# The product with w_in in seven half products, on a normed stream kept on chip as seven blocks

## The chip, the cores and the metric

The kernel runs on one core of one Trainium2 chip. The metric is the device time of one launch in microseconds (us). Every float32 product is made on TensorE (PE) from two rounded halves of each operand, a high part `hi` and a low remainder `lo`, as three matmuls: hi by hi, hi by lo, lo by hi.

## The reference

One encoder block over 1040 positions (16 learned meta tokens ahead of 1024 frames) of width 1024. Eight heads stand side by side: heads 0 to 3 are mLSTM heads, heads 4 to 7 retention heads. Each needs q and k (128 wide), v and an output gate o (256 wide), and all are columns of one product with `w_in`.

```python
up   = rmsnorm(h, norm_mix_g)                  # h: meta tokens and x, 1040 x 1024
proj = up @ w_in                               # 1024 x 6152
q, k = silu(causal_dwconv(...)) or rotary(...) # per head, 128 wide
h_ml = sigmoid(ml_o) * head_norm(mlstm_chunkwise(q, k, v, gates))
h_rt = silu(rt_g)    * head_norm(retention_chunkwise(q, k, v))
h = h + concat(h_ml, h_rt) @ w_out             # 2048 x 1024
h = h + channel_mixer(rmsnorm(h, norm_ffn_g))  # w_up, w_gate, conv, w_down; 2816 wide
out = rmsnorm(h, norm_final_g)[16:]
```

## The kernel before, in words

Activations lie with the features on the partitions: 8 blocks (`KB`) of 128 features by 1040 positions. The code is traced once in Python, fully unrolled; a planner then orders the instructions of each engine by its own costs, by data dependences and by hand-written order edges (`after`). Semaphores are made from that.

**The stream.** `resid` (8 blocks, float32) is loaded once and stays on chip for the whole kernel. `gained` multiplies it by the norm's gain and splits it into `uh` and `ul`, four pieces of positions at a time (`NP`). The 1/rms of each position is not multiplied in there: it is applied where a product is taken out of PSUM, as `Rb` (a row per position) for q, k and o, and as `Rc`, `Rg`, `Rk` (a column per position) for v and in the scan. So PE can start before the norm of a piece is known.

**The product with w_in.** It goes head by head in the order `HEADS` = 4, 0, 1, 2, 3, 5, 6, 7. Weights come as units of 128 x 1024 (or 1056 for the first v): `issue` (L129) loads a unit by SP's queue into one of two raw buffers, ACT makes `hi` (L145) and DVE `lo` (L146), in one of three buffers; `need` asks for a unit and two ahead of it.

- `v_group` (L411 to 434) makes v with positions on the partitions, one chunk of 128 positions at a time: 8 blocks x 3 matmuls of 256 columns (L431 to 433). The 16 meta positions are a small float32 product of their own (L420). `v_evac` writes `vh` and `vl` (L406, L407).
- `fm_mms` (L436 to 443) makes q, k and the two halves of o with features on the partitions, in three pieces of 400, 384 and 256 positions. `qk_group` finishes a piece of q or k on the way out of PSUM: a convolution of four taps and SiLU for mLSTM heads (L462 to 468), the rotation for retention heads (L470 to 473). `o_group` (L483, L484) applies the sigmoid or SiLU.
- `gates` works the gate rows of all mLSTM heads out once, after head 4's v; `tables` brings them, or the rotation's tables, into `A1` and `A2`.

**The scan.** Each head runs over nine chunks (16 positions, then eight times 128): `scan_a` (L842 on) makes scores, `scan_b` (L882 on) the chunk's output and the carried state, `post_steps` the head's norm and the product with the gate. These pieces are laid by `merge` between the products of the same head's o and the next head's v:

```python
for i, h in enumerate(HEADS):
    merge([... o_group(h, b, p) ...], [A(0)] + [B(c) for c in range(4 if i < 7 else NCH)])
    ...
    merge([lambda c=c: v_group(g, c)() for c in range(NCH)], side)   # g: the next head
    tables(g)
    for kind in "qk":
        for p in range(3):
            qk_group(g, kind, p)
```

**After it.** The products with `w_out`, `w_up`, `w_gate` and `w_down` are each made in seven half products in place of eight already (`Seven`, `seven`), in which sums of weight quarters and of activation blocks stand for the quarters themselves. For `w_out` those sums are made on DVE by `wsum` (L185) during heads 1 to 7 and stored to DRAM; for `w_down` by `dload`, `dsum` and `dstep` (L198 to 234), on DVE, during the products with w_up and w_gate. Two positions at the end of the sequence fall outside the halves; `last_two` (L173) adds their share of w_out on DVE into `acc` (L178).

PSUM has eight banks: three `pp`, two `sA`, and one each of `num`, `upd` and `tr`.

Of the kernel before, what the change touches and what calls it, by code (L numbers as in the profile page):

```python
# [35 lines left out]
UN = 4 * 264  # L36
# [6 lines left out]
FIRST = HEADS[0]  # L43
PIECES = [(0, 400, (0, 1, 2, 3)), (400, 784, (4, 5, 6)), (784, 1040, (7, 8))]
WMAX = 400
# [19 lines left out]
def body(ctx, tc, h_in, vecs, cst, mask_in, rot, w_v0, w_v, w_fm, w_out, w_up, w_gate, w_down, out):  # L65
# [9 lines left out]

    def after(later, first):

        tc.add_manual_dep(later.ins, first.ins.name, mybir.DependencyInfo(mybir.DependencyClass.NoSync, mybir.DependencyReason.DATA),
                          reason="order")
# [5 lines left out]
    resid = per.tile([P, KB, T], F32, name="resid")  # L85
    upool = ctx.enter_context(tc.tile_pool(name="upool", bufs=1))
    ublk = [tuple(upool.tile([P, 2 * T], F32R, tag=f"u{x}{i}", name=f"u{x}{i}") for x in "hl") for i in range(4)]
    uh, ul = ([ublk[kb // 2][x][:, (kb % 2) * T:(kb % 2 + 1) * T] for kb in range(KB)] for x in (0, 1))
    accseg = ExitStack()
    accp = accseg.enter_context(tc.tile_pool(name="accp", bufs=1, side="right"))  # L90

    acc = accp.tile([P, 2, D], F32, name="acc")
    mm = accp.tile([P, 2 * 8, 2], F32, name="mm")
    rring = []
# [3 lines left out]
    epsc = per.tile([P, 1], F32, name="epsc")  # L98
    Rb = per.tile([P, T], F32, name="Rb")

    ident = cs[:, C_ID:C_ID + P]

    NP = [(0, 144), (144, 400), (400, 784), (784, 1040)]
    nc.scalar.dma_start(vec, vecs)
    for kb in (0, 4):
        nc.sync.dma_start(resid[:, kb:kb + 4, 0:144], h_in[:, kb:kb + 4, 0:144])
    nc.vector.memset(epsc, EPS)
    nc.scalar.activation(Rb[:, 0:1], epsc, AF.Square)

    PSB = {"pp": 3, "sA": 2, "num": 1, "upd": 1, "tr": 1}  # L110

    def pp(name, tag="pp"):
        return ps.tile([P, 512], F32, tag=tag, name=name, bufs=PSB[tag])

# [5 lines left out]
    def unit(key, src, n):  # L120
        units.append((key, src, n))
# [7 lines left out]
    def issue(upto):  # L129
        while issued[0] < min(upto, len(units)):  # L130
            u = units[issued[0]]
            issued[0] += 1
            if callable(u[1]):
                ready[u[0]] = u[1]()
                continue
            key, src, n = u
            nm = "_".join(str(k) for k in key)
            raw = raw_tile(nm)
            sub = 2 if key[:2] == ("v", FIRST) else 1
            cuts = [n * i // sub for i in range(sub + 1)]  # L140
            for c0, c1 in zip(cuts, cuts[1:]):
                nc.sync.dma_start(raw[:, c0:c1], src[:, c0:c1])
            hi, lo = split_tiles(nm)
            for c0, c1 in zip(cuts, cuts[1:]):
                x = (nc.scalar.copy(hi[:, c0:c1], raw[:, c0:c1]),  # L145
                     nc.vector.tensor_tensor(lo[:, c0:c1], raw[:, c0:c1], hi[:, c0:c1].bitcast(F32), ALU.subtract))  # L146
                if key[:2] in (("k", FIRST), ("o", FIRST)):
                    for a, b in zip(x, last["evac"]):
                        after(a, b)
            ready[key] = (hi, lo, raw)  # L150
# [8 lines left out]


    def u_v(h):
        for half in range(2):
            if h == FIRST:
                unit(("v", h, half), w_v0[half], 4 * 264)
            else:
                unit(("v", h, half), w_v[h - (h > FIRST), half], 4 * 256)

    def u_f(h, kind):
        j = {"q": 0, "k": 1, "o": 2}[kind]
        for b in range(2 if kind == "o" else 1):  # L170
            unit((kind, h, b), w_fm[h, j + b], D)

    def last_two(k, raw=None):  # L173
        raw = raw_tile(f"m{k}") if raw is None else raw
        nc.sync.dma_start(raw[:, :D], w_out[k])
        for t in range(2):
            if k != 2 * FIRST:
                nc.vector.scalar_tensor_tensor(acc[:, t], raw[:, :D], mm[:, k, t:t + 1], acc[:, t], ALU.mult, ALU.add)  # L178
            else:
                nc.vector.tensor_scalar(acc[:, t], raw[:, :D], mm[:, k, t:t + 1], None, ALU.mult)  # L180


    sums = {(g, st, k): dram.tile([P, 2 * HB], F32, name=f"ws{g}{st}_{k}") for g, n in (("w", 8), ("d", KD)) for st in ("65", "73") for k in range(n)}

    def wsum(g, k):  # L185
        src, n = (w_out, 8) if g == "w" else (w_down, KD)
        a, b = (accp.tile([P, 2 * HB], F32, tag=f"rr{i}", name=f"ws{g}{k}_{i}") for i in range(2))
        nc.sync.dma_start(a, src[k])
        nc.sync.dma_start(b, src[k + n])
        w11, w21, w12, w22 = a[:, :HB], a[:, HB:], b[:, :HB], b[:, HB:]  # L190
        after(nc.vector.tensor_tensor(w22, w21, w22, ALU.add), last["qk"])
        nc.vector.tensor_tensor(w21, w21, w11, ALU.subtract)
        nc.vector.tensor_tensor(w11, w22, w11, ALU.subtract)
        nc.vector.tensor_tensor(w12, w12, w11, ALU.subtract)
        for st, i, x in (("65", 0, w11), ("65", 1, w22), ("73", 0, w12), ("73", 1, w21)):
            nc.sync.dma_start(sums[g, st, k][:, i * HB:(i + 1) * HB], x)

    def dload(k, q, x):  # L198

        n = HB // 2  # L200
        b = x.rearrange("p (a b j) -> p a b j", a=2, b=2)
        for i in range(2):
            nc.sync.dma_start(b[:, :, i], w_down[k + i * KD].rearrange("p (a j) -> p a j", a=2)[:, :, q * n:(q + 1) * n])

    def dsum(k, q, x, prev):

        n = HB // 2
        w11, w12, w21, w22 = (x[:, i * n:(i + 1) * n] for i in range(4))
        after(V.tensor_tensor(w22, w21, w22, ALU.add), prev)
        V.tensor_tensor(w21, w21, w11, ALU.subtract)  # L210
        V.tensor_tensor(w11, w22, w11, ALU.subtract)
        V.tensor_tensor(w12, w12, w11, ALU.subtract)
        for st, i, j in (("65", 0, 4), ("73", 1, 3)):
            nc.sync.dma_start(sums["d", st, k].rearrange("p (a j) -> p a j", a=2)[:, :, q * n:(q + 1) * n],
                              x.rearrange("p (i j) -> p i j", i=4)[:, i:j:3 if st == "65" else 1])

    dcount = [0, 0]
    dunits = [(k, q) for k in range(KD) for q in range(2)]
    dbufs = []

    def dnext():

        if len(dunits) > dcount[1]:
            x = dbufs[dcount[1] % 2] or fp4.tile([P, 2 * HB], F32, tag="dsum", name=f"dsum{dcount[1]}", bufs=1)
            dopen.append((*dunits[dcount[1]], x))
            dload(*dopen[-1])
            dcount[1] += 1

    dopen = []

    def dstep(x):
        if dopen:
            dsum(*dopen.pop(0), x)
            dnext()


# [4 lines left out]
    def first_right(k):  # L241
        a = accp.tile([P, 2 * HB], F32, tag="rr0", name=f"fr{k}")
        r = accp.tile([P, 2 * HB], F32R, tag="rr1", name=f"frs{k}")
        nc.sync.dma_start(a, mxd[k])
        nc.scalar.copy(r[:, :HB], a[:, :HB])
        after(nc.vector.tensor_tensor(r[:, HB:], a[:, :HB], r[:, :HB].bitcast(F32), ALU.subtract), last["qk"])
        nc.vector.tensor_tensor(a[:, HB:], a[:, HB:], a[:, :HB], ALU.subtract)
        nc.sync.dma_start(rone[k], r.bitcast(F32))
        nc.sync.dma_start(diff[k], a[:, HB:])

    ahead = {(g, "q", 0): [lambda k=k: wsum("w", k)] for k, g in enumerate((1, 2, 3, 5, 6, 7))}
    for k, g in ((6, 6), (7, 7)):
        ahead[g, "k", 1] = [lambda k=k: wsum("w", k)]
    for k in range(8):
        ahead[5 + k // 3, *(("q", 1), ("q", 2), ("k", 0))[k % 3]] = [lambda k=k: first_right(k)]

    def u_m(h):
        for b in range(2):
            units.append((("m", h, b), lambda k=2 * h + b: last_two(k)))

    def u_vqk(h):
        u_v(h)
        u_f(h, "q")
        u_f(h, "k")

    u_vqk(FIRST)
    for i, h in enumerate(HEADS):
        u_f(h, "o")
        if i:
            u_m(HEADS[i - 1])  # L270
        if i < 7:
            u_vqk(HEADS[i + 1])


# [57 lines left out]
    def gained(kb, t0, t1, gcol, dve=False):  # L332
        g = vec[:, gcol + kb:gcol + kb + 1]
        if dve:
            nc.vector.tensor_scalar(uh[kb][:, t0:t1], resid[:, kb, t0:t1], g, None, ALU.mult)
        else:
            nc.scalar.activation(uh[kb][:, t0:t1], resid[:, kb, t0:t1], AF.Copy, scale=g)
# [234 lines left out]
    def tables(h):  # L572
        if h > H + 1:
            return
# [16 lines left out]

    HALF = SEQ // 2
    QT = HALF // 2  # L600

# [1082 lines left out]
```

## Time and profile before

| | us |
|---|---|
| median of 3 runs | 1538.67 (1537.11 to 1539.1) |
| span of the profiled execution | 1536.0 |
| busy in it: PE, DVE, ACT, POOL | 1512.7, 1131.5, 743.2, 2.5 |
| product with w_in and the scans | about 0 to 690 of the span |
| product with w_out | about 690 to 870 |
| products with w_up and w_gate | about 870 to 1305 |
| product with w_down and the last norm | about 1305 to 1536 |

The profiled execution has no time of its own beside its span; the span runs from the first to the last instruction, and the median of the runs lies 2.7 us above it. In a row of a group of instructions stand line, engine, operation, output and inputs, shape and count, then busy time, mean nanoseconds of one, and the idle time before it with what ended it. PEld is the loading of weights into PE, beside its matmuls. A line such as L146 is a line of the kernel before.

### The profile page before, as it was taken

The page shows a single profiled execution, that of the slowest core. Times are in us where ns is not written, and L with a number is a line of the kernel's source. Part 1 is how long each engine was busy: PE and PEld are TensorE (multiplying, and loading weights), DVE is VectorE, ACT ScalarE, POOL GpSimd, SP SyncE. Part 2 cuts the span into 40 slices and gives each one's busy share as a digit, 9 for nine tenths or more (in the row PEclk, how much of TensorE's full clock was granted, in tenths as well). Part 3 has the DMA queues.
Part 4 walks back from the last instruction along what each step waited for, and adds up shares of the span by engine and source line. Part 5 has one row for each costly group of instructions (what it writes and reads, how often), then busy time and mean ns, then how long its engine had stood idle before and what let it go on. Part 6 is the DMA issues. An engine that isn't in the chain of part 4 may idle for free.

```text
span 1536.0 us, 25538 instructions
## 1 busy us (share of the span) xinstructions
PE 1512.7 (98%) x9753; PEld 1392.8 (91%) x9753; DVE 1131.5 (74%) x2443; ACT 743.2 (48%) x1491; POOL 2.5 (0%) x13
## 2 busy tenths in 40 slices
PE   7999999999999999999999999999999999999997
PEld 7989999999999999998788998999999999888887
DVE  8757767686867677687966788677777777778657
ACT  7374555555542534434454465444444444344443
POOL 0000000000000000000000000000000000000000
PEclk9999999999999999999999999999999999999999
DMA  6131231332425346278542245323465656933313
GB/s 216 42 98 63 70 122 65 109 112 80 141 67 184 126 131 209 91 249 305 184 146 97 83 129 181 102 93 101 155 193 167 198 186 230 366 109 104 96 42 111
DMA packets 111771, 213.18 MB, mean 139 GB/s; under 512 B 9944, under 2 KB 54688, under 8 KB 111648
## 3 DMA queue, kind: packets, MB, share of 16 engines
q1 hardware_dynamic: 111504, 211.48, 41.8%
q8 instruction: 76, 1.25, 0.3%
q14 instruction: 47, 0.39, 0.1%
q10 hardware_dynamic: 144, 0.07, 0.0%
HBM read 155.89 MB, written 55.62 MB: 138 GB/s over the span
## 4 chain that ended last, share of the span: by engine, by line
PE 95%; DMA 2%; DVE 2%; ACT 1%; issue 0%; DVEq 0%; ACTq 0%
PE pv L431 4%; PE pv L432 4%; PE pv L433 4%; PE po L442 4%; PE po L441 4%; PE po L443 4%; PE pdx L608 3%; PE pdx L610 3%; PE pdx L609 3%; PE pup_x L609 2%; PE pup_x L610 2%; PE pga_x L608 2%; PE pga_x L610 2%; PE pga_x L609 2%; PE pup_x L608 2%; PE pdy L608 2%
## 5 line engine op out<-in xcount | busy, mean ns | idle before, releaser
L431 PE MATMUL pv<-hi_v,uh 128*128 128x256 f32 (+1 forms) x512 | 147.2, 288 | 7.7 <-ACT hi_v L145 7.7
L432 PE MATMUL pv<-lo_v,uh 128*128 128x256 f32 (+1 forms) x512 | 145.9, 286 | 0.0
L433 PE MATMUL pv<-hi_v,ul 128*128 128x256 f32 (+1 forms) x512 | 145.6, 285 | 0.0
L441 PE MATMUL po<-uh,hi_o 128*128 128x386 f32 (+2 forms) x384 | 125.1, 326 | 0.0
L442 PE MATMUL po<-ul,hi_o 128*128 128x386 f32 (+2 forms) x384 | 122.8, 320 | 0.0
L443 PE MATMUL po<-uh,lo_o 128*128 128x386 f32 (+2 forms) x384 | 122.6, 319 | 0.0
L431 PEld LDWEIGHTS pv<-hi_v,uh 128*128 128x128 f32 x512 | 97.2, 190 | 10.5 <-ACT hi_v L145 7.7
L432 PEld LDWEIGHTS pv<-lo_v,uh 128*128 128x128 f32 x512 | 96.9, 190 | 0.9 <-DVE lo_v L146 0.8
L433 PEld LDWEIGHTS pv<-hi_v,ul 128*128 128x128 f32 x512 | 96.9, 190 | 0.1
L299 ACT CAST hi_up<-raw_up 128x512 fp32r<-128x512 f32 (+1 forms) x52 | 36.5, 719 | 105.7 <-PE pga_z L609 60.7
L441 PEld LDWEIGHTS po<-uh,hi_o 128*128 128x128 f32 x384 | 72.5, 189 | 0.1
L442 PEld LDWEIGHTS po<-ul,hi_o 128*128 128x128 f32 x384 | 72.4, 189 | 0.1
L443 PEld LDWEIGHTS po<-uh,lo_o 128*128 128x128 f32 x384 | 72.2, 188 | 0.1
L608 PE MATMUL pup_x<-uh_g,hi_up 128*128 128x256 f32 (+1 forms) x240 | 67.2, 282 | 0.4 <-ACT uh_g L1096 0.4
L609 PE MATMUL pup_x<-ul_g,hi_up 128*128 128x256 f32 (+1 forms) x240 | 67.4, 283 | 0.1
L610 PE MATMUL pup_x<-uh_g,lo_up 128*128 128x256 f32 (+1 forms) x240 | 66.3, 282 | 0.0
L300 DVE TENSOR_TENSOR lo_ga<-fraw_ga,hi_ga 128x512 fp32r<-128x512 f32 (+1 forms) x52 | 41.9, 808 | 32.2 <-ACT hi_ga L299 32.1
L300 DVE TENSOR_TENSOR lo_d<-rd,hi_d 128x1024 fp32r<-128x1024 f32 (+1 forms) x34 | 37.7, 1112 | 34.8 <-ACT hi_d L299 34.8
L441 PE MATMUL pq<-uh,hi_q 128*128 128x400 f32 (+2 forms) x192 | 62.1, 323 | 1.0 <-DVE qT L472 0.9
L442 PE MATMUL pk<-ul,hi_k 128*128 128x400 f32 (+2 forms) x192 | 62.1, 324 | 0.0
L441 PE MATMUL pk<-uh,hi_k 128*128 128x400 f32 (+2 forms) x192 | 62.0, 323 | 0.0
L443 PE MATMUL pq<-uh,lo_q 128*128 128x400 f32 (+2 forms) x192 | 62.0, 323 | 0.0
(757 smaller groups left out, 4978.7 us busy)
## 6 DMA issues: line engine op xcount, KB each, us to landing
raw_up<-w_up_d SPq DMA_DIRECT2D x22, 512.0 KB, 3.6
fraw_ga<-w_gate_d SPq DMA_DIRECT2D x22, 512.0 KB, 4.5
acts<-cv SPq DMA_DIRECT2D x44, 256.0 KB, 3.5
rd<-wsd SPq DMA_DIRECT2D x22, 512.0 KB, 3.5
raw_o<-w_fm_d SPq DMA_DIRECT2D x16, 512.0 KB, 3.5
wsw<-w_out_d SPq DMA_DIRECT2D x16, 512.0 KB, 3.8
wsw<-wsw SPq DMA_DIRECT2D x32, 256.0 KB, 2.1
raw_v<-w_v_d SPq DMA_DIRECT2D x14, 512.0 KB, 3.7
```

Of the source, the lines that this page charges most:

```text
L299: nc.scalar.copy(hi[:, o:o + n], x)
L300: nc.vector.tensor_tensor(lo[:, o:o + n], x, hi[:, o:o + n].bitcast(F32), ALU.subtract)
L431: nc.tensor.matmul(pv[:L, :nv], a, hi[:, o:o + nv], start=kb == 0, stop=False)
L432: nc.tensor.matmul(pv[:L, :nv], a, lo[:, o:o + nv], start=False, stop=False)
L433: nc.tensor.matmul(pv[:L, :nv], b, hi[:, o:o + nv], start=False, stop=kb == KB - 1)
L441: nc.tensor.matmul(pt[:, :n], a, uh[kb][:, t0:t1], start=kb == 0, stop=False)
L442: nc.tensor.matmul(pt[:, :n], a, ul[kb][:, t0:t1], start=False, stop=False)
L443: nc.tensor.matmul(pt[:, :n], b, uh[kb][:, t0:t1], start=False, stop=kb == KB - 1)
L608: m.append(nc.tensor.matmul(pt, ah, xh_, start=first and k == 0, stop=False, skip_group_check=True))
L609: nc.tensor.matmul(pt, ah, xl_, start=False, stop=False, skip_group_check=True)
L610: m.append(nc.tensor.matmul(pt, al, xh_, start=False, stop=last and k == n - 1, skip_group_check=True))
```

## The change

The product with w_in is put into seven half products, like the four others. Its input features are halved (4 blocks each), its output columns are halved, and the positions are halved into two stretches of `SB` = 528 (the second begins at position 512, so 16 positions are made twice). With X11 to X22 the four blocks of the normed stream (position half, feature half) and S1 to S4 sums of them, each of seven products takes one block and one quarter, or sum of quarters, of the weights.

```diff
+    ROWS = [("x", "11", 0, 0), ("y", "12", 0, 1), ("x", "S2", 1, 0), ("y", "S1", 1, 1), ("x", "S3", 2, 1), ("y", "S4", 3, 0), ("x", "22", 2, 0)]
+    def wino_fm(kind, h, chunks, dst):
+        get = gbanks(f"{kind}{h}")
...
+        for n, (b, xb_, ui, hf) in enumerate(ROWS):
+            for ci, (j0, j1) in enumerate(chunks):
...
+                    hi, lo, _ = need((kind, h, ui), 2)
...
+                    mm3s(pt, [tuple(x[:, hf * HB + k * P:hf * HB + (k + 1) * P] for x in (hi, lo)) for k in range(4)],
+                         [tuple(x[:, k, j0:j1] for x in u) for k in range(4)], n in (0, 1, 3), n in (1, 5, 6))
...
+                    if n in (0, 6):
+                        nc.scalar.copy(d, q)
+                    elif n in (2, 3):
+                        nc.scalar.activation(d, q, AF.Copy, scale=-1.0)
+                    else:
+                        last["pace"] = V.tensor_tensor(d, d, q, ALU.add if n == 1 else ALU.subtract)
...
+    FMC = [(0, 264), (264, SB)]
+    OC = [(KEEP, 272), (272, SB)]
```

q and k of a head are the two column halves of one group (`qk_steps`), the two halves of o of another (`o_steps`). v is made for two heads of `PAIRS` = (0, 1), (2, 3), (5, 6) in one group (`v_steps`: four pairs of 128 positions, 256 columns each); head 7's v is a group with features on the partitions (`v7_steps`) and is transposed back per chunk (`v_split`). Head 4, the first, keeps v, q and k as plain products (`v4_group`, `q4_group`); its o is a group. q and k land as `raws`, and `qk_final` does the convolution or rotation from there; v stays in float32 and `v_split` splits it into `hi` and `lo` chunk by chunk, in the scan.

The stream is normed before it is split. `first_norm` takes five stretches in turn; after the last, the sums are made in place of blocks that are no longer needed:

```diff
+        for i, x in enumerate(xs):
+            for k in range(4):
+                V.scalar_tensor_tensor(x[:, k], x[:, k], vec[:, V_MIX + 4 * i + k:V_MIX + 4 * i + k + 1], pr, ALU.mult, ALU.mult)
+            h_, l_ = (u[:, :, j0:j1] for u in UB[f"{half + 1}{i + 1}"])
+            nc.scalar.copy(h_, x)
+            last["pace"] = V.tensor_tensor(l_, x, h_.bitcast(F32), ALU.subtract)
...
+    usum(0, "22", "21", "S1")
+    usum(0, "11", "21", "21")
+    usplit("S3", "21", "r0", "r1")
+    usum(1, "S1", "11", "11")
+    usum(1, "11", "12", "12")
+    usplit("S4", "12", "r2", "r3")
+    usplit("S2", "11", "uh2", "ul2")
+    usplit("S1", "S1", "uh3", "ul3")
```

The seven blocks fill the room of `resid`; so x is loaded a second time, ahead of the product with w_out, into `RT`.

Sums of weight quarters are made in DRAM by adding DMAs of POOL's queue (GpSimd's), for w_in (`insum`), w_out and w_down (`wsum`), in place of DVE's sums; `job` issues an insum at the start of each group, two groups ahead of its use. `last_two` scales on ACT and adds into DRAM:

```diff
+    def wsum(g, k):
...
+        for x, y in ((d65, src[k]), (d73[:, HB:], v21), (d73[:, :HB], v12)):
+            dep(G.dma_start(x, y), last["pace"], True)
+        add(d65[:, HB:], v22)
+        add(d73[:, HB:], v11)
+        add(d65[:, :HB], d65[:, HB:])
+        add(d73[:, :HB], d65[:, :HB])
+    def insum(w, q, n, cuts):
+        for i in range(cuts):
+            c = 4 * n // cuts
+            dep(G.dma_start(q[:, i * c:(i + 1) * c], w[:, i * c:(i + 1) * c]), last["pace"], True)
+        b = lambda x, o: x[:, o * n:(o + 1) * n]
+        add(b(q, 1), b(w, 3))
+        add(b(q, 3), b(w, 0))
+        add(b(q, 0), b(q, 1))
+        add(b(q, 2), b(q, 0))
...
+            nc.scalar.activation(x, raw, AF.Copy, scale=mm[:, k, t:t + 1])
...
+                G.dma_start(accd[t], x, accum_op=ALU.add)
```

The order around it: each group of products (`group`) takes some of the scan's pieces of the head before.

```diff
+    for p, (a, b) in enumerate(PAIRS):
+        group(qk_steps(a), 7)
+        steps, meta = v_steps(p)
+        group(steps[:12], 99, 0, 10)
+        tables_load(a)
+        meta()
+        qk_final(a)
+        tables_make(a)
+        side += tasks(a)
+        if p:
+            wsum("w", wjobs.pop(0))
+        merge(steps[12:], take(5), 6)
+        group(o_steps(a), 5)
...
+        group(qk_steps(b), 99)
...
+        qk_final(b)
+        tables_make(b)
+        side += tasks(b)
+        group(o_steps(b), 5, 5)
```

The banks of PSUM become two `pa`, two `pb` and one each of `sA`, `num`, `upd` and `tr`. Signs of the sums in the later products are turned so that DMAs need only add.

More of the change, by code (lines that the diff above doesn't have):

```diff
@@ L191, in wsum @@
[L191 to L203, printed above, removed]
@@ L217, in body @@
[L217 to L234, printed above, removed]
+        d65, d73 = sums[g, "65", k], sums[g, "73", k]
@@ L1087, in body @@
+    wsum("w", wjobs.pop(0))
+    group(qk_steps(7), 7)
+    wsum("w", wjobs.pop(0))
+    steps = v7_steps()
+    group(steps[:6], 99)
+    tables_load(7)
+    qk_final(7)
+    vtile[7] = [vslot(i, f"n7_{i}") for i in range(2)]
+    merge(steps[6:], [lambda: scan_a(7, 0)], 6)
+    merge(o_steps(7), [ab(7, c) for c in range(NCH)])
+    issue(len(units) - len(fu))
     TA, TB = KEEP, KEEP + XW - 2
```

949 lines of the change are left out of this document (554 added, 395 removed).

## The prediction

> **What bounds the kernel now.** The page first.
>
> ```profile
> span 1536.0 us, 25538 instructions
> ...
> PE 1512.7 (98%) x9753; PEld 1392.8 (91%) x9753; DVE 1131.5 (74%) x2443; ACT 743.2 (48%) x1491; POOL 2.5 (0%) x13
> ...
> PE 95%; DMA 2%; DVE 2%; ACT 1%; issue 0%; DVEq 0%; ACTq 0%
> ```
>
> PE is busy for 98% of the span and carries 95% of the chain that ended last. A busy PE may still be a slow one, so the second view splits the span by stage. Columns: stretch and length, then PE, weight loads, DVE, ACT and POOL, then granted clock, DMA share and GB/s.
>
> ```profile
> 0.00:64.50 64.50, 55.14 (x390) 52.71 (x391) 51.09 (x133) 35.90 (x89) 1.06 (x11) 1.00 0.44 153
> 64.50:98.30 33.80, 33.01 (x227) 30.15 (x224) 17.43 (x57) 23.46 (x42) 0.00 (x0) 1.00 0.30 90
> 98.30:182.30 84.00, 82.36 (x597) 81.16 (x597) 61.08 (x174) 44.87 (x99) 0.00 (x0) 1.00 0.16 53
> 182.30:266.50 84.20, 84.20 (x617) 82.45 (x619) 61.79 (x172) 48.04 (x103) 0.00 (x0) 1.00 0.32 101
> 350.70:434.90 84.20, 84.20 (x617) 82.45 (x619) 61.69 (x170) 45.38 (x100) 0.00 (x0) 1.00 0.31 101
> 603.90:690.00 86.10, 86.10 (x632) 84.28 (x633) 64.85 (x161) 36.60 (x88) 0.00 (x0) 1.00 0.52 169
> ```
>
> The first 690 us hold the product with w_in and the scans of the eight heads. One head takes 84.2 us with PE full and the clock at 1.00, while DVE works 61.8 us of it, ACT 48.0 and POOL nothing. So this stage falls with the columns that PE must stream. The pace of a product is read from starts in the timeline, since the duration of a matmul includes its pipeline.
>
> ```profile
> 184.67 0.28 PE L431 MATMUL pv<-hi_v,uh 128*128 128x256 f32 x1
> ...
> 189.85 0.28 PE L433 MATMUL pv<-hi_v,ul 128*128 128x256 f32 x1
> ```
> ```profile
> 226.61 0.34 PE L441 MATMUL pk<-uh,hi_k 128*128 128x400 f32 x1
> ...
> 230.81 0.34 PE L443 MATMUL pk<-uh,lo_k 128*128 128x400 f32 x1
> ```
>
> The first pair is the ends of 45 matmuls: 44 steps in 5.18 us, 0.1177 us each, 0.460 ns a column. The second is 24 matmuls: 23 steps in 4.20 us, 0.1826 us, 0.457 ns. Width does not matter between 256 and 400; I use 0.459 ns.
>
> **Columns removed.** Each exact product is three matmuls (high by high, high by low, low by high). Before, a head streams for q and k 2 x 24 x 1040 = 49920 columns (24 = 8 blocks x 3), for the gate output o 2 x 24 x 1026 = 49248, for v 8 x 24 x 256 = 49152: 148320, or 68.1 us of the 84.2. The remaining 16.1 us are scan, transposes and the 16 meta rows, which stay. After, a group is seven half products of 4 blocks x 3 = 12 matmuls: q with k 7 x 12 x 528 = 44352, o 7 x 12 x 514 = 43176, v of two heads 7 x 12 x 4 x 256 = 86016, so 43008 a head. That is 130536; 17784 fewer for each of heads 0, 1, 2, 3, 5 and 6. Head 7 makes v as a group of 44352 columns: 16440 fewer. Head 4, the first, keeps plain v, q and k and saves 6072 on o. Sum 106704 + 16440 + 6072 = 129216 columns x 0.459 ns = **59.3 us off PE**.
>
> **Added to PE.** Head 7's v comes out transposed and is turned back by 18 transposes.
>
> ```profile
> 196.57 0.64 PE tr L956 x4
> ```
>
> Four cost 0.64 us, so 18 cost 2.9 us. **+3**
>
> **The first head.** Before, the stream goes into PE raw and its norm is multiplied in afterwards. Now each of five stretches must be squared, summed, normed, scaled and split first; then four sums of blocks (S1 to S4) must be made and split before o of head 4 can pass its second row of products.
>
> ```profile
> 3.97 0.54 ACT L1028 ACTIVATE qT<-resid 128x144 f32<-128x144 f32 x2 [1.28 <-DMA resid<-h_in_d]
> ...
> 7.65 0.59 PE L431 MATMUL pv<-hi_v,uh 128*128 128x264 f32 x1 [7.65 <-ACT hi_v L145]
> ```
> ```profile
> L441 PE MATMUL po<-uh,hi_o x384: 275/337/427, 64.5 to 688.3; 128*128 128x386 f32 x64, 128*128 128x384 f32 x64, 128*128 128x256 f32 x64
> ```
> ```profile
> L146 DVE TENSOR_TENSOR lo_o<-raw_o,hi_o 128x1024 fp32r<-128x1024 f32 x16 | 19.5, 1218 | 1.0 <-ACT hi_o L145 0.9
> L145 ACT CAST hi_o<-raw_o 128x1024 fp32r<-128x1024 f32 x16 | 16.8, 1048 | 13.1 <-PE pq L442 12.0 <-PE pv L433 1.1
> ```
>
> Before, the first matmul starts at 7.65 us and o of head 4 at 64.5, though its v and q, k need only (50688 + 49920) x 0.459 = 46.2 us: 18 us of the start are other work and waits. After: x lands at 3.97. At about 1.2 ns an element on DVE and 1.05 on ACT (the two rows), the first 144 columns take 1.3 us of squares, 1.4 of sums, an estimated 2 for the root and its spread over partitions, 1.2 of scaling and 1.4 of split: 7.3 us, so products begin near 11.5, 4 us later. A stretch of 256 columns costs DVE 2.1 us of sums, 3.8 of scaling and 2.4 of low halves, 8.3 us, and feeds PE with 24 x (2 x 264 + 2 x 256) x 0.459 = 11.5 us of products; PE soon sets the pace and ends q, k of head 4 near 65. The sums cost DVE 8 sums + 8 low halves of 1056 elements at 1.25 us, 20 us, from about 52 on; o of head 4 has 5.7 us of ready rows. It waits from 71 to about 74. The gates and the rotation of head 4 follow on DVE before its scan may begin; I let them lie beside the 14 us of o that are left. I take **+6**, ends 0 (the old waits already cover it) and +16 (none overlaps).
>
> **Steady work on DVE and ACT.** Weight units rise from 6 x 1024 elements a head to 10.5 x 1024 (3.5 for q with k, 3.5 for o, 3.5 for v): +4.5 x 1.218 = +5.5 us DVE, +4.5 x 1.048 = +4.7 us ACT.
>
> ```profile
> L178 DVE SCALAR_TENSOR_TENSOR acc<-raw_m,mm,acc 128x1024 f32<-128x1024 f32 x26 | 32.2, 1278 | 0.0
> L407 DVE SCALAR_TENSOR_TENSOR vl<-pv,Rg,vh 128x256 fp32r<-128x256 f32 x32 | 15.4, 481 | 6.7 <-ACT vh L406 6.3
> L1329 ACT COPY s0up<-pup_x 128x258 f32<-128x258 f32 x10 | 3.8, 375 | 2.0 <-PE pup_x L610 2.0
> ```
>
> The sums for the last two rows (4 x 1.278 = 5.1 us of DVE a head) go to ACT (4 x 1.05 = +4.2) and to adding DMAs of POOL's queue. Emptying a group is 8 ACT copies (0.375) and 6 DVE adds (about 0.48): for three groups +9 us ACT, and 8.6 us DVE in place of about 10 (20 passes). v is split anew per chunk: 9 x 0.375 on ACT, 9 x 0.48 on DVE. ACT: 48 + 4.7 + 4.2 + 9 + 3.4, less some 4 of the old v emptying, is about 65 of a period of 76; DVE: 61.8 + 5.5 - 5.1 - 1.4 + 4.3, about 65. Neither is over PE, but ACT goes from 57% to 85%, and PSUM banks and the single raw pair of q, k tie each group to the last one's emptying. In the stage rows above PE idles 0.8 us, 1.6 us and then nothing from head to head; I add **+8** for new waits, ends 0 and +25.
>
> **POOL's queue.** Sums of weights are made in DRAM by 19 insum chains and 8 wsum chains, on a queue that before moved almost nothing.
>
> ```profile
> q1 hardware_dynamic: 111504, 211.48, 41.8%
> ...
> q10 hardware_dynamic: 144, 0.07, 0.0%
> ...
> wsw<-wsw SPq DMA_DIRECT2D x32, 256.0 KB, 2.1
> ...
> raw_v<-w_v_d SPq DMA_DIRECT2D x14, 512.0 KB, 3.7
> ...
> wsd<-Rb SPq DMA_DIRECT2D x22, 256.0 KB, 5.4
> ...
> resid<-h_in_d SPq DMA_DIRECT2D x2, 1024.0 KB, 7.5
> ```
>
> No row shows an adding DMA, nor one from DRAM to DRAM. A chain is one copy of 1 MB, then adds of 256 KB of which three must follow one another. Bounds for one add: 2.1 us (a store alone) and 12.8 (two loads at 3.7 and a store at 5.4). I take 4.5, nearest to the 512 KB load, which moves as much as the two operands. A chain is then 7.5 + 3 x 4.5 = 21 us; the doubled chain for v about 28, a wsum about 17. Pair 1 or 2 asks for 4 x 21 + 28 + 3 x 17 + 4 x 4.5 = 181 us if nothing overlaps, in a period of 152 on PE. The demand is 51.7 + 28.7 x (one add). Over two such pairs, less a lead of two groups (some 40 us), PE would be held by 2 x (181 - 152) - 40 = 18 us. Independent chains can fill each other's waits, so I book nothing, but this is the thin place. A job's copies also wait for an emptying on DVE; behind them on POOL stand all later jobs and the adds of the last two rows, whose source is one of three weight buffers, so a late add holds back the next weights too.
>
> The Trainium skill ("DMA: Bandwidth & Descriptors", section on the SWDGE path) fits a POOL-issued DMA as 2.0 us + bytes / 436 GB/s; by that an add of 256 KB is an estimated 2.6 us, a pair 111 us, and nothing waits. No run here shows it yet; the sum is the same by either.
>
> **What else moves.** The w_down sums leave DVE for POOL.
>
> ```profile
> 870.00:1305.00 435.00, 434.40 (x2806) 395.26 (x2805) 330.05 (x604) 206.84 (x392) 0.00 (x0) 1.00 0.48 154
> ```
>
> DVE is off the chain there (PE 434.4 of 435), so 0; 11 chains of 17 us are 190 of those 435, and if they end late, w_down's third step waits for them. x is loaded a second time before w_out on SP's queue, under head 7's scan: 4 MB at four rows of 7.5 us, 30 us, cover is w_out's first rows; 0, or +5 if exposed.
>
> **Sum** against the profiled span: 1536.0 - 59.3 + 3 + 6 + 8 = 1493.7. The runs shown have a median of 1538.67, 2.7 above that span, so **1496.4 us**. A measurement of this kernel can tell 0.2% (3.1 us) from no change.
>
> **Rivals.** *POOL's chains come late* (0.24). The w_in weights wait in `issue` for sums; PE stands at rows S2 to S4 of each group. For: serial demand of 181 against 152. Against: an idle queue and the lead. At 6 us an add the pair asks 51.7 + 28.7 x 6 = 224, 72 over; two pairs less 40 of lead give +104: 1496 + 104 = **1600**. With nothing overlapped it decides from 4.9 us an add: 193 a pair, 2 x 41 - 40 = 42, the whole gain.
>
> *In-order waits eat half* (0.15): ACT at 85% copies a bank late, or the start costs its upper end: +16 and +25 in place of 6 and 8 give **1523**, still faster. For: hi_o idles 13.1 us in its row above, 12.0 of it behind one engine's buffer. Against: with the same scan PE idles nowhere in the rows from 182.3 and 350.7.
>
> *The columns do not set the pace* (0.06): the emptying of seven products on ACT and DVE binds instead and the stage keeps its 84 us; **1538**, no change. Against: 65 of 76.
>
> **Numbers.** Forecast 0.55, range of its own 1474 to 1516 (start and waits at 0 give 1482 and unforeseen ends elsewhere 8 less; +18 to +20 above). Faster 0.55 + 0.15 = 0.70; same 0.04 (most of the last rival); slower 0.26 (POOL, and the rest). Cutting 0.05 below and some 0.15 above, the range is 1474 to 1572.
>
> **What would show it.** Right: period of a pair near 152 us with PE full; the stage ends near 645; first matmul near 11 to 13; ACT near 85% there; POOL's DMAs landing at 3 to 5 us. Wrong: PE waiting on ACT `hi` behind a DMA whose source is a sum (POOL); PE waiting on DVE S1 to S4 or on qk_final beyond 10 us (start); a period over 160 with banks named as releasers (emptying).

## The result and the profile after

The changed kernel takes 1701.85 us (median of 3 runs, 1695.37 to 1706.06) where the kernel before takes 1538.67: 1.106 times as long, interval 1.1023 to 1.1097. The forecast was 1496.4, with a range up to 1572. In one execution below (`e1_no_pool_sums`, 1943.0 us) the granted clock was 0.64 to 0.75 from end to end, as in no other, so its time is not compared with anything and the kernel was run again.

The page of after, its busy times, granted clock, POOL's DMA queue and the chain that ended last:

```profile
span 1704.1 us, 26448 instructions
...
PE 1543.8 (91%) x9999; PEld 1398.7 (82%) x9999; DVE 1104.5 (65%) x2322; ACT 836.3 (49%) x1658; POOL 192.0 (11%) x270
...
PEclk8999899799989989889879999999999999999999
...
q0 software_dynamic: 30656, 99.63, 28.9%
...
PE 63%; DMA 20%; issue 6%; DVE 6%; ACT 4%; POOL 1%; SPq 1%; DVEq 0%; POOLq 0%; ACTq 0%
```

PE carried 95% of the chain before; now it carries 63%, and DMA 20%. POOL's queue moves 99.63 MB and takes 28.9% of the DMA engines' time; the page of before has no such row. The granted clock lies below nine tenths in 9 of the first 21 slices. The windows, cut where the three pairs of heads, head 7, `w_out` and w_up start, say which stage lost (columns as in the prediction's windows):

```profile
113.30:329.70 216.40, 180.58 (x1315) 167.03 (x1315) 120.46 (x347) 124.19 (x268) 24.88 (x32) 0.90 0.67 166
329.70:525.40 195.70, 167.67 (x1287) 158.36 (x1285) 115.66 (x332) 118.57 (x255) 38.03 (x51) 0.94 0.84 205
525.40:731.00 205.60, 172.02 (x1275) 160.81 (x1274) 113.31 (x295) 90.16 (x205) 43.90 (x58) 0.92 0.88 217
731.00:866.60 135.60, 107.96 (x725) 99.81 (x724) 80.82 (x218) 72.15 (x166) 17.00 (x23) 0.83 0.94 286
866.60:1080.60 214.00, 214.00 (x1174) 185.75 (x1173) 160.44 (x283) 100.90 (x189) 0.00 (x0) 0.98 0.40 129
```

A pair of heads takes 216.4, 195.7 and 205.6 us where 152 was forecast (and two heads took 168 before). PE is idle for 28 to 36 us of each, the clock is at 0.90 to 0.94, and the DMA share is 0.67 to 0.88 where the prediction's rows of single heads have 0.16 to 0.52. `w_out` starts at 866.6 in place of 689.5: 177 us later, more than the whole loss of 168.1 between the spans (1704.1 against 1536.0). From there on nothing is lost.

The DMA issues of after, from 60 to 866 us (KB each, median us from issue to landing):

```profile
raw_o<-gs SPq DMA_DIRECT2D x15, 512.0 KB, 7.2
raw_q<-gs SPq DMA_DIRECT2D x14, 512.0 KB, 4.5
gs<-w_g_d POOLq DMA_DIRECT2D x28, 256.0 KB, 7.4
gs<-gs POOLq DMA_DIRECT2D x28, 256.0 KB, 6.8
...
accd<-hi_m POOLq DMA_DIRECT2D x13, 512.0 KB, 8.0
accd<-lo_m POOLq DMA_DIRECT2D x13, 512.0 KB, 9.4
...
raw_q<-w_g_d SPq DMA_DIRECT2D x7, 512.0 KB, 6.8
```

An adding DMA of 256 KB lands after 6.8 to 7.4 us (4.5 was taken), one of 512 KB out of a weight buffer after 8.0 to 9.4. And the loads of 512 KB on SP's queue, 3.5 to 4.6 us for w_in before, take up to 7.2, whether they read a sum (`gs`) or plain weights (`w_g_d`). A piece of the chain that ended last shows one way in which this reaches PE (start, us, what):

```profile
199.91 5.91 DMA gs<-w_g_d
...
206.22 7.44 DMA gs<-w_g_d
...
222.47 15.72 issue
238.22 0.90 POOL accd L243
...
239.25 11.22 DMA accd<-lo_m
250.55 1.24 DVE lo_q L202
251.83 0.39 PE pq1y L452
```

POOL works a chain of sums off, and only behind it the add of the last two rows (L243) whose source is a weight buffer. (For the 15.72 us of "issue" between them the profile names no wait.) When that add has landed, DVE may write the next low half `lo_q` into the buffer, and PE goes on. PE itself waits 2.1 us for this `lo_q`: its idle time from 113 to 866 us is spread over many short waits, the largest sums being 13.6 us in 5 waits for `vm`, the loads of v's weights for the 16 meta rows, and 12.4 us in 5 waits for `den`, a piece of the scan that DVE makes.

### The profile page after: what moved, and what is told of

The parts are those of the page before. It is cut to its first block, busy times and chain, and to the rows that moved or that the text cites. A ratio compares the mean times of both kernels' runs of the same rounds, so it can differ in the third digit from the quotient of the medians.

```text
span 1704.1 us, 26448 instructions
## 1 busy us (share of the span) xinstructions
PE 1543.8 (91%) x9999; PEld 1398.7 (82%) x9999; DVE 1104.5 (65%) x2322; ACT 836.3 (49%) x1658; POOL 192.0 (11%) x270
## 3 DMA queue, kind: packets, MB, share of 16 engines
q0 software_dynamic: 30656, 99.63, 28.9%
## 4 chain that ended last, share of the span: by engine, by line
PE 63%; DMA 20%; issue 6%; DVE 6%; ACT 4%; POOL 1%; SPq 1%; DVEq 0%; POOLq 0%; ACTq 0%
DMA accd<-lo_m 2%; DMA A<-scr 2%; PE pdx L450 2%; PE pdx L451 2%; PE pdx L452 2%; PE pup_x L451 2%; PE pga_x L451 2%; PE pup_x L452 2%; PE pup_x L450 2%; PE pga_x L452 2%; PE pga_x L450 2%; DMA gs<-w_g_d 2%; PE pwx L451 2%; DMA diff<-raw_fr 2%; PE pwx L450 2%
## 5 line engine op out<-in xcount | busy, mean ns | idle before, releaser
L355 DVE TENSOR_TENSOR lo_up<-raw_up,hi_up 128x512 fp32r<-128x512 f32 (+1 forms) x52 | 41.3, 810 | 36.1 <-ACT hi_up L354 35.2
L354 ACT CAST hi_ga<-fraw_ga 128x512 fp32r<-128x512 f32 (+1 forms) x52 | 36.4, 719 | 45.0 <-PE pup_z L451 22.9
L451 PE MATMUL pdx<-ul_d,hi_d 128*128 128x512 f32 (+1 forms) x156 | 58.1, 375 | 0.0
L452 PE MATMUL pdx<-uh_d,lo_d 128*128 128x512 f32 (+1 forms) x156 | 57.6, 373 | 0.0
L451 PE MATMUL pdy<-ul_d,hi_d 128*128 128x512 f32 x132 | 51.9, 393 | 0.0
L452 PE MATMUL pdy<-uh_d,lo_d 128*128 128x512 f32 x132 | 51.3, 389 | 0.0
L450 PE MATMUL pdx<-uh_d,hi_d 128*128 128x512 f32 (+1 forms) x156 | 48.8, 374 | 0.0
L450 PE MATMUL pdy<-uh_d,hi_d 128*128 128x512 f32 x132 | 48.3, 392 | 0.0
L451 PE MATMUL pga_x<-ul_g,hi_ga 128*128 128x512 f32 x120 | 47.6, 397 | 0.0
L452 PE MATMUL pga_x<-uh_g,lo_ga 128*128 128x512 f32 x120 | 47.3, 394 | 0.0
```

Source lines behind the costliest of these rows:

```text
L354: nc.scalar.copy(hi[:, o:o + n], x)
L355: nc.vector.tensor_tensor(lo[:, o:o + n], x, hi[:, o:o + n].bitcast(F32), ALU.subtract)
L450: m.append(nc.tensor.matmul(pt, ah, xh_, start=first and k == 0, stop=False, skip_group_check=True))
L451: nc.tensor.matmul(pt, ah, xl_, start=False, stop=False, skip_group_check=True)
L452: m.append(nc.tensor.matmul(pt, al, xh_, start=False, stop=last and k == n - 1, skip_group_check=True))
```

## The experiments

Two theories stood at first. **Late sums**, the recorded rival: products wait for sums that POOL's queue makes too slowly. **The rest of the rewrite**: start, in-order waits and copies out of PSUM cost the time, whatever POOL does. Later a third came up, **crowding**: POOL's DMAs slow the other transfers, whoever reads the sums. Unless an interval is given, a time is of a single run; the three runs of the changed kernel lie within 10.7 us, so a few us between single runs say nothing. The kernel before ran beside each on the same chip; its medians there lie between 1536.06 and 1539.19.

**All of POOL's sums out** (for w_in, for `w_out`, and for the last two rows; plain quarters of w_in and plain rows of `w_out` are loaded in their place).

```diff
-        w, q = w_g[i], gsum[i]
+        w = q = w_g[i]
...
-        w, q = w_vp[p], vsum[p]
+        w = q = w_vp[p]
...
-            else:
-                G.dma_start(accd[t], x, accum_op=ALU.add)
...
-        src, n = (w_out, 8) if g == "w" else (w_down, KD)
+        if g == "w":
+            return
+        src, n = w_down, KD
...
     def insum(w, q, n, cuts):
+        return
...
-                nc.sync.dma_start(x[:, :2 * HB], sums[self.nm, st, k])
+                nc.sync.dma_start(x[:, :2 * HB], w_out[k + 8 * (st == "73")] if self.nm == "w" else sums[self.nm, st, k])
```

> Left out, all on POOL's queue and all before the product with w_out ends: the insum chains (units load plain quarters of w_in in place of the sums), the wsum chains of w_out (plain rows of w_out are loaded) and the adds of the last two rows into DRAM. Everything on PE, DVE and ACT stays. Theory A (POOL's adding DMAs hold the stage): 1500 us, at most 1530, a pair near 152 us. Rival B (the normed start and in-order waits between ACT, DVE and PE hold it): above 1620. In between, both have a share, and the distance to 1500 is B's.

The repeat:

> The same kernel as e1_no_pool_sums again, since that one ran at a granted clock of 0.65 to 0.75 from its first slice to its last and its time can't be compared. If the low clock belongs to this kernel (PE without pauses), it returns, and the time is 1900 again. If it was the chip's, A expects 1490 to 1530 and B above 1600; e1's PE waited only 9 us between 100 and 800, but for a slower PE all others are faster.

Measured: 1563.57 (1561.38 to 1565.76), 1.0176 times the kernel before, interval 1.0142 to 1.0211. So POOL's sums cost 138 us, and the rest of the rewrite alone is already slower than before, 67 us above the forecast. Its windows, cut at the same places:

```profile
0.00:66.00 66.00, 44.91 (x297) 42.39 (x298) 43.48 (x97) 30.67 (x47) 0.57 (x11) 0.90 0.39 127
66.00:109.20 43.20, 40.87 (x328) 40.16 (x327) 34.99 (x56) 21.19 (x34) 0.00 (x0) 0.96 0.22 68
109.20:297.60 188.40, 172.54 (x1316) 160.35 (x1315) 124.04 (x352) 125.93 (x270) 0.00 (x0) 0.95 0.34 108
297.60:459.60 162.00, 155.74 (x1268) 148.60 (x1267) 111.24 (x318) 118.55 (x250) 0.00 (x0) 1.00 0.40 120
459.60:615.90 156.30, 156.30 (x1281) 149.79 (x1280) 116.67 (x306) 95.32 (x212) 0.00 (x0) 1.00 0.44 139
615.90:725.90 110.00, 95.05 (x739) 89.06 (x737) 79.29 (x221) 68.31 (x164) 0.00 (x0) 0.95 0.77 271
```

The last pair has PE full at full clock and takes 156.3 us, 4 above the 152 of the forecast. The loss lies at the two ends: a start with 23 of 109 us idle, a first pair with 16 of 188, and head 7 with 15 of 110.

**One kind of sum out at a time**, each by its part of that diff. First the sums for w_in (products read plain quarters):

> Only the 19 insum chains are left out (units load plain quarters of w_in). Theory A in its first form (the sums of w_in come late themselves): POOL keeps 3 wsum chains and 4 to 8 adds a pair, some 150 us in 152, so 1520 to 1570. In its second form (the adds of the last two rows stand on POOL's queue and keep a weight buffer): they now find a shorter queue, so 1560 to 1620. Rival B: above 1650.

Then the adds of the last two rows (the two rows lack all but one of their shares):

> Only the adds of the last two rows into DRAM are left out (their ACT scaling and their weight buffers stay, so a buffer is free as soon as ACT is done). First form of A: 1640 to 1680, since an insum chain is as long as before. Second form (buffers kept): 1540 to 1600. Rival B: above 1680.

Then the sums for `w_out` (plain rows are loaded):

> Only the 8 wsum chains of w_out are left out (plain rows of w_out are loaded in the later product). A counted as one serial queue: some 85 us a pair less in pairs 1 and 2, so 1560 to 1620. If pairs wait for the length of a single chain and not for the queue's load: 1680 to 1700, since pair 0 has no wsum and took as long as the others. Rival B: 1700.

And only these left in:

> Left out: the insum chains (plain quarters loaded) and the adds of the last two rows; the 8 wsum chains of w_out stay on POOL. Nothing that PE waits for in this stage is then behind POOL. Theory A: 1500 to 1540. Rival B (start, in-order waits): 1600 or more, close to the 1624 of the kernel without insum.

Measured: without the sums for w_in 1624.29 (78 less than after), without the adds of the last two rows 1654.65 (47 less), without the sums for `w_out` 1647.59 (54 less); with the sums for `w_out` alone 1580.56, which is 17 above none. The three savings add up to 179, not 138, and the sums for `w_out` are worth 17 alone and 54 beside the others: each kind makes the others dearer.

**The chains' copies start without waiting** for PE's progress:

```diff
-            dep(G.dma_start(x, y), last["pace"], True)
+            dep(G.dma_start(x, y), last["pace"], False)
...
-            dep(G.dma_start(q[:, i * c:(i + 1) * c], w[:, i * c:(i + 1) * c]), last["pace"], True)
+            dep(G.dma_start(q[:, i * c:(i + 1) * c], w[:, i * c:(i + 1) * c]), last["pace"], False)
```

> The first copies of each chain no longer wait for an emptying on DVE (the edge stays as an order for the planner, without a wait); nothing else changes and nothing is left out. POOL waited for such edges some 180 us in the profile of after. If the loop 'POOL waits for DVE, DVE for PE, PE for weights, weights for POOL' is the cost: 1580 to 1640. If POOL's own load is: 1680 to 1700. If earlier copies only crowd the DMA engines: above 1700.

Measured: 1748.78, 47 us slower. If products waited for late sums, starting the chains earlier should have helped. That it hurt fits crowding, but the run doesn't show by which way it hurt.

**The sums are made, and not read.** All chains run as in the changed kernel; the products with w_in read plain quarters.

```diff
-        w, q = w_g[i], gsum[i]
+        w = q = w_g[i]
...
-        w, q = w_vp[p], vsum[p]
+        w = q = w_vp[p]
```

> All sums are issued as in the changed kernel, on the same queue at the same times, but the products with w_in read plain quarters of the weights in place of the sums (these values are left wrong); the sums for w_out are read as before. If POOL's chains cost time because the products wait for them (lateness), the run comes out near the one without these sums, 1624 us, with the waits of gs and vs on their copies unchanged and PE's waits gone. If they cost time because their traffic slows the other transfers (contention), it stays near 1702. Halfway, about 1660, would be both. I expect 1640: most of it lateness, some left because the adds for the last two rows still queue behind the unread chains and hold a weight buffer.

Measured: 1702.59, against 1701.85 with the sums read. I had expected 1640, and late sums lost its main support: with all of POOL's work in place, reading the sums costs no time that shows. (A wait for a sum could still hide behind another wait on the same queue; the pair of runs below takes the other two kinds out.) The loads of plain quarters are as slow as those of sums were (DMA issues from 0 to 870 us):

```profile
raw_o<-w_g_d SPq DMA_DIRECT2D x24, 512.0 KB, 7.1
raw_q<-w_g_d SPq DMA_DIRECT2D x22, 512.0 KB, 6.4
```

In the kernel without POOL's sums the same loads, from 60 to 860 us, take

```profile
raw_q<-w_g_d SPq DMA_DIRECT2D x21, 512.0 KB, 3.7
raw_o<-w_g_d SPq DMA_DIRECT2D x21, 512.0 KB, 4.0
```

**Only the chains for w_in, unread and read.** The other two kinds are out; the first of the two runs has the diff above as well.

> Of POOL's sums in this stage only the 19 chains for w_in are left, and no product reads them (plain quarters are read; the adds of the last two rows and the sums of w_out are left out, so values are wrong). No buffer and no product waits for POOL's queue, so all that the time lies above 1563.6 us is what this traffic does to the other transfers. If contention is the main way of the loss, 1620 or more; if the held weight buffers are, 1580 or less. I expect 1590, with the 512 KB loads of w_in landing in 5 to 6 us against 3.7 to 4.0 without POOL's sums.

> The same, but the products read the sums (adds of the last two rows and sums of w_out left out, so values are wrong). The difference to the run before it is the lateness of the sums alone, free of the other two kinds of POOL's work. If products wait for chains, it is 20 us or more; since reading the sums made no difference with all of POOL's work in place (1702.59 against 1701.85), I expect less than 8 us.

Measured: 1599.17 unread, 1596.65 read. Traffic that nobody waits for costs 1599.17 - 1563.57 = 35.6 us; reading its results adds nothing (2.5 less, of single runs). The loads of 512 KB of w_in land after 4.5 to 5.1 us in the unread run, from 60 to 800 us, against the 3.7 to 4.0 above.

**The same traffic in the kernel before**, 21 chains on POOL's queue, unread. Each is two copies of 512 KB and four adds of 256 KB, DRAM to DRAM, and they start with the q of a head:

```diff
+            if key[0] == "q" and key[1] != FIRST:
+                for j in range(3):
+                    chain(key[1], j)
```

> The kernel before, with 21 chains added on POOL's queue, three a head, each of 1 MB copied and four adds of 256 KB from one DRAM place to another; nobody reads them. If such traffic slows any kernel's loads, the time rises by some 20 us or more, as the 19 chains cost the changed kernel 35.6 us; if it hurts only where the loads have no lead, it stays within 8 us of before, because there the weights are loaded well ahead of PE. I expect the loads of q, o and v to go from 3.5 to about 5 us and the time to rise by 5 us.

Measured: 1572.69, against 1537.58: 35.1 us. I had expected 5, since this kernel keeps PE full and its loads run ahead. The price is nearly the one in the changed kernel, so it belongs to the traffic and not to the rewrite. The DMA issues from 60 to 740 us:

```profile
raw_v<-w_v_d SPq DMA_DIRECT2D x12, 512.0 KB, 9.9
raw_q<-w_fm_d SPq DMA_DIRECT2D x7, 512.0 KB, 6.6
raw_k<-w_fm_d SPq DMA_DIRECT2D x7, 512.0 KB, 7.9
```

The waits of the same kernel (total us, times, longest), ACT's first and then PE's:

```profile
ACT hi_v L158 <- DMA raw_v<-w_v_d: 38.5, 10, 7.4
```
```profile
PE pv L444 <- ACT hi_v L158: 8.0, 1, 8.0
PE u L891 <- ACT kwh L872: 6.2, 2, 3.2
PE u L891 <- ACT kwh L883: 5.5, 2, 3.2
PE n L891 <- ACT num L925: 5.3, 2, 4.4
```

The load of v's weights goes from 3.7 us to 9.9; that of o's, later in a head, stays at 3.6 (3.5 before). ACT stands at `hi_v` until the weights are there: 38.5 us in 10 waits, where it was 16.8 in 8. PE's waits are on `kwh` and `num`: pieces of the scan that ACT makes, which need no weights at all. The first wait was there before (7.7 us); the next three total 17 us, where the trace of before has less than 1 us on each. The timeline of the longest wait on `kwh` shows how the two hang together, ACT first and then PE:

```profile
448.02 1.05 ACT L158 CAST hi_v<-raw_v 128x1024 fp32r<-128x1024 f32 x1 [7.41 <-DMA raw_v<-w_v_d]
...
450.38 0.42 ACT L481 ACTIVATE kT<-cvk 128x256 f32<-128x256 f32 x1
...
452.11 0.52 ACT L497 ACTIVATE sig<-sig 128x384 f32<-128x384 f32 x1
452.54 0.35 ACT L872 ACTIVATE kwh<-s,cols 128x128 fp32r<-128x128 f32 x1
```
```profile
452.94 0.39 PE L891 MATMUL u<-vh,kwh 128*128 128x258 f32 x1 [3.22 <-ACT kwh L872]
```

ACT stands 7.4 us for the late load, then works off what stands in its order, `kwh` among it, and PE starts as soon as `kwh` is there: the scan stands behind a late load in ACT's order. Four of the waits in these three rows, 12.9 of the 17 us, follow such a stand of ACT, three for `raw_v` and one for `raw_q`; one of 3.2 us follows a wait for a table (`A`). The whole loss adds up from the page of this run: PE idles 43.5 us of the span in place of 23.3, and is busy for 1527.4 us in place of 1512.7, at a mean clock of 0.987 in place of 0.996; together 34.9. The instructions themselves are not slower beside the chains (DVE's `lo_o` of 1024 columns takes 1218 ns in both kernels); it is the transfers that grow. Whether the DMA engines or the memory behind them run short, no run separates.

**Adds as plain copies**, same bytes, order and waits:

```diff
-        return G.dma_start(x, y, accum_op=ALU.add)
+        return G.dma_start(x, y)
...
-                G.dma_start(accd[t], x, accum_op=ALU.add)
+                G.dma_start(accd[t], x)
```

> Every adding DMA on POOL's queue becomes a plain copy of the same bytes with the same source, target, order and waits (sums are left wrong). If accumulating is what makes a transfer dear, landings fall from 6.4 to 9.4 us to about 4 and the time falls by most of the 138 us that the sums cost, to about 1600. If the price is POOL's issuing and the way from DRAM to DRAM, landings stay above 6 us and the time within 25 us of 1702. By my recorded formula, 51.7 + 28.7 x (one add), an add of 5 us gives 195 a pair and 1538 to 1580; I expect landings of 5 to 6 us and 1640.

Measured: 1627.22, 75 us less (1640 expected). Landings from 60 to 790 us:

```profile
gs<-w_g_d POOLq DMA_DIRECT2D x28, 256.0 KB, 5.5
gs<-gs POOLq DMA_DIRECT2D x28, 256.0 KB, 4.5
accd<-hi_m POOLq DMA_DIRECT2D x13, 512.0 KB, 5.5
accd<-lo_m POOLq DMA_DIRECT2D x13, 512.0 KB, 6.7
```

Each lands 1.9 to 2.7 us sooner than the add in its place. Adding makes up a bit more than half of what the sums cost; the traffic as such makes up the rest.

**The last two rows' adds without the weight buffer.** The source is DRAM in place of the buffer, at the same place in the queue.

```diff
-                G.dma_start(accd[t], x, accum_op=ALU.add)
+                dep(G.dma_start(accd[t][:, :D - 1], w_out[k][:, :D - 1], accum_op=ALU.add), a, True)
```

> The changed kernel, but each add for the last two rows takes its source from DRAM (w_out itself, not yet scaled, one column short, so these two rows are wrong) in place of the weight buffer; it starts at the same place in the queue, after the same scaling on ACT, and moves the same bytes. The traffic stays, the held buffer goes. Leaving these adds out altogether gave 1654.65, 47 us less. If the held buffer is the way of that loss, the run comes to about 1655 to 1665; if their traffic and their time on the queue are, it stays within 10 us of 1702. I expect 1665.

Measured: 1678.97. Of the 47 us that these adds cost, 23 go with the held buffer, and 24 stay with the traffic and the time on the queue (single runs; the adds from DRAM land after 9.4 us, no sooner than those from the buffer).

**The table of constants ahead of the stream**, in the kernel without POOL's sums:

```diff
+    nc.sync.dma_start(cs, cst)
     xload(0)
...
-    nc.sync.dma_start(cs, cst)
```

> The kernel without POOL's sums in this stage (1563.6 us), with the table of constants loaded ahead of the stream in place of behind its first part and the first weights; the sums are left out, so values are wrong. If the late start is that one load (PE waited 9.1 us for it), the column sums begin 2 to 4 us earlier and the first product starts near 13 in place of 16.5; the run comes out near 1560. If the norm's own chain (squares, sums, root, scaling on DVE and ACT) sets the start, the first product stays within 1 us of 16.5 and the time stays at 1563. I expect 1561: a small part of the loss at the start; the waits for the later stretches (DVE x, u21h, u11l) and the half clock after them stay.

Measured: 1566.35 (1566.22 to 1566.48), against 1563.57: nothing gained. PE's wait for that table (9.1 us) was only the last of several. With the table early, PE waits for the squares in its place (PE's waits to 66 us, then its first work):

```profile
PE pca L399 <- DVE sqr L427: 11.2, 2, 9.9
```
```profile
17.46 0.59 PE L440 MATMUL pv<-w0hiq,u11h 128*128 128x264 f32 x1 [1.16 <-ACT u11h L433]
```

But the run doesn't settle what sets the start: with the table ahead of it the stream itself comes later, and ACT's second squares start at 7.52 us in place of 5.00. What both runs share is the way from the first column sums on PE to the first product: 9.09 to 16.53 us without the edit, 9.88 to 17.46 with it, 7.4 and 7.6 us. No run led to a version that beats the kernel before: even the kernel without any of POOL's sums in this stage is slower.

## Why the prediction was wrong, and where it was right

**Columns removed: right in the main.** Where nothing disturbs it (last pair without POOL's sums) a pair falls from 168 us to 156.3 with PE full at full clock, 12 of the 16 us forecast. The pace held: the median step there is 0.118 us for 256 columns and 0.122 for 264, 0.461 and 0.462 ns a column against 0.459. Where the other 4 us lie is not broken down.

**POOL's queue: wrong, and this is the step that failed.** The prediction asked only whether the sums would come in time, found a demand of 181 us in a period of 152, and booked nothing. Two things failed in it. The price: an add was taken at 4.5 us and measured 6.8 to 7.4. The Trainium skill ("DMA: Bandwidth & Descriptors", section on the SWDGE path) has 2.0 us + bytes / 436 GB/s, which gives an estimated 2.6; the adds of these runs take 2.6 to 2.8 times that, and plain copies of the same size 4.5 to 5.5 us. And, weighing more, the mechanism: the question was put to the queue alone, while its traffic slows the transfers beside it (loads of 3.7 to 4.0 us take 6.4 to 7.1) and so the engines that stand behind them in order. The forecast's sum had no term for that at all. Unread traffic costs 35.6 us in the changed kernel and 35.1 in the kernel before. The same page of the Trainium skill states, in its section "Issuing engines are not separate DMA queues", that DMAs started by any engine run on the same 16 DMA engines and interleave; both runs agree, and the prediction did not use it.

**The rival on POOL's queue: right direction, wrong reason.** At 7.2 us an add (the median of `gs<-w_g_d` over the whole trace) its formula gives 51.7 + 28.7 x 7.2 = 258 a pair, 2 x (258 - 152) - 40 = 172 us, and 1668, near the 1701.85. That is luck: the pairs took 196 to 216 us, not 258, and the sums unread gave the same time, so the waits it describes did not set it. What it said of the adds of the last two rows, that a late one holds back the next weights, did occur; the held buffer is worth some 23 us.

The 138 us, put on one at a time: chains for w_in 35.6 (1563.57 to 1599.17), reading them nothing, the sums for `w_out` beside them 58 (1596.65 to 1654.65, the run without the adds of the last two rows), and those adds 47 (1654.65 to 1701.85). Alone the sums for `w_out` cost 17, so some 41 of their 58 is what two kinds of chains do to each other. How much of that, and of the 24 that these adds cost beside the held buffer, is slowed loads and how much a longer queue is open.

**The start (+6): too little.** The first product starts at 16.9 us in after and 16.5 without POOL's sums; 11.5 was forecast. The way from the column sums to the first product, 7.4 us, was taken at 4.6 (2 for the root and its spread, 1.2 and 1.4), and the column sums stand until 9.1 for the table of constants. To the start of q of head 0, without POOL's sums, PE idles 23.4 us of 109.2 and runs at a clock of 0.90 and 0.96, which costs an estimated 44.91 x 0.10 + 40.87 x 0.04 = 6 us more. Before, it idled 10 us to 98.3 at full clock.

**New waits (+8): too little.** Without POOL's sums the three pairs idle 22 us and head 7 another 15; by the same estimate the clock costs 8.6 and 4.8 us there. In head 7's stretch the scan has few products left beside it. Above the kernel before, start and pairs lose some 19 and 28 us, about the upper ends on record (+16 and +25); head 7 comes on top. The longest of head 7's waits, 5.6 us, is PE's for the first weights of `w_out`. All in all PE idles 60 us to the start of `w_out`, where it idled 13 before, and the clock costs some 20: 67 more, of which 14 were booked. That is 53 of the 81 us between the 645 forecast for this mark and the 725.9 of this run. The rest lies in stretches that count as busy; if each pair lacks the 4 us of the last one, 13 of it are columns that were saved less than forecast, and what is left is not broken down.

**The clock: not foreseen.** The prediction's windows show 1.00 throughout, and it took PE's pace as fixed. After a wait PE comes back at half pace. In after PE waits 2.7 us for `v4hi`, to 182.79, and then 1.2 us more (a window of 5 us, then the timeline):

```profile
185.00:190.00 5.00, 2.63 (x10) 1.50 (x8) 5.00 (x13) 4.53 (x10) 0.00 (x0) 0.50 0.35 105
```
```profile
191.76 0.41 PE L451 MATMUL pv0y<-lo_vp,uS4h 128*128 128x256 f32 x1
191.97 0.41 PE L452 MATMUL pv0y<-hi_vp,uS4l 128*128 128x256 f32 x1
192.19 0.41 PE L450 MATMUL pv0y<-hi_vp,uS4h 128*128 128x256 f32 x1
```

0.215 us a step of 256 columns, in place of 0.1177. An idle microsecond thus costs more than itself. The Trainium skill ("TensorE: Matmul & The Clock Gate", Part 1) says that an idle window of about 3.4 us halves the array's clock until a busy one has passed; the clock of 0.50 agrees.

**Steps that held.** The emptying on ACT: a pair without POOL's sums has 126, 119 and 95 us of ACT, 63 to 48 a head, where 65 was worked out; the period did not stay at 84. The sums of w_down on POOL cost nothing: w_up's start to w_down's is 395.9 us, of which PE is busy 394.57 (394.6 and 394.00 before). `w_out`'s own stretch takes 214.0 us where it took 221 (689.5 to 910.7; the table ahead of the prediction ends it near 870, too early).

**The second load of x: open.** It was booked at 0, or 5 if exposed. Without POOL's sums its eight loads are issued from 692.5 to 705.5 us, and land after 7.0 to 10.4. The first weights of `w_out`, issued behind them at 716.35, land 8.4 us later, and the wait of 5.6 us above is for these, where the trace of before has none. How much of it is the load of x, among the other transfers of that stretch (a DMA share of 0.77), no run says.

## What to carry to other kernels

Work that is moved from an engine to DMAs is paid in part by the transfers that run beside it: price its bytes, reads and writes and copies together, against the loads that the kernel lives on, and then ask which engine stands in order behind those loads. Here 35 us were lost in a kernel whose PE was 98% busy, to transfers that nobody read. To tell lateness from crowding, run the work and don't read its result. And price waits of PE above their length: here it came back from them at half clock.

## What the runs showed of the hardware

- An adding DMA of 256 KB from DRAM to DRAM lands after 6.8 to 7.4 us, the same transfer as a plain copy after 4.5 to 5.5. One of 512 KB from SBUF takes 8.0 to 9.4, as a copy 5.5 to 6.7.
- A load of 512 KB on SP's queue goes from 3.7 us to as much as 9.9 when POOL's DMAs run beside it, while DVE's instructions keep their length (`lo_o`, 1218 ns).
- After waits of some microseconds PE streams 256 columns in 0.215 us in place of 0.1177, and the mean granted clock of the whole run falls with it, from 0.996 to 0.946.
